# Experts taken in the order of their token counts, two or four to a step, with register-addressed weights

## The chip, the cores and the metric

One core of a Trainium2 chip runs the whole program. The metric is the device time of one launch in microseconds. Its engines are TensorE (PE; its weight loads are listed as PEld), VectorE (DVE), ScalarE (ACT), GpSimd (POOL) and SyncE (SP). All weights are fetched from memory by DMAs that SP issues.

## What the reference computes

Two transformer blocks on 512 tokens of width 1024, in float32. The first has attention and a mixture of experts, the second two kinds of mixing and a dense feed-forward part. The change lies in the mixture of experts:

```python
pg = softmax(hf @ wg + bg); gsel = argmax(pg); pg_sel = max(pg)      # 1 of 4 groups
le = (hf @ we + be).reshape(n, 4, 8)[gsel]                           # 8 experts of that group
p_top, e_loc = top_k(softmax(le), 2)                                 # 2 experts per token
gate = pg_sel * p_top / sum(p_top)
# each of the 32 experts on its tokens:
y = (silu(x @ w1[e]) * (x @ w3[e])) @ w2[e]     # w1, w3: 1024 x 512, w2: 512 x 1024
out[token] += gate * y
```

512 tokens with two experts each are 1024 rows for 32 experts, 32 on average, in numbers that depend on the data. Every expert's weights are 3 x 2 MB, all experts' 201 MB.

## The kernel before

`phase1` does attention. `phase2`, from L835, projects, routes, runs the experts and hands over to the second block (`project2`, `phase3`).

*Routing.* For each of four token tiles `route` finds the two experts. `Ab` marks token and expert. A matmul with a triangle of ones counts, so `rk` (L922) holds a token's place among its expert's tokens, 1 upwards, and 0 where it isn't there; `rt` holds the gates, `rs` their high and low halves. Places make one-hot matrices `G` (L956): column s of an expert is 1 at the token with place s + 1. `gather` (L959) multiplies the normed tokens, held as high and low halves, with `G` and leaves the expert's inputs in `xg`, 64 columns (slots) per expert.

*Steps.* 16 steps (L1052) take two experts each in the order of their numbers. `expert_pair` (L1155) multiplies by `w1` and `w3` (L1174), the first expert's 64 rows of output in partitions 0 to 63, the second's in 64 to 127: each matmul loads 64 columns of `xg` and streams 512 columns of weights. Silu, product and gate (L1181), transposes (L1185), `w2` (L1195). The result goes back to its tokens by a matmul with another one-hot matrix `pm` in the next step (`back`, L1203 to L1210). The list `todo` puts work on the next experts between the parts of a step: in every step half of the next gather, 256 columns wide for two steps, and the two halves of `back`.

*Weights.* `expert` (L179) cuts each matrix into two halves and so issues twelve DMAs of 1 MB per step from SP (L188), into a ring of 14 slots of 1 MB (`NW2`). SP issues in program order; a DMA waits until the matmuls that last read its slot are done. The addresses are fixed, so nothing but slots holds them back: those of step 0 and two of step 1 go out while the routing still runs.

*Leftovers.* An expert with more than 64 tokens is finished by the loop at L1094, one block of 64 slots per pass, with its own gather and weight load. `table` (L1010) lists the blocks; it runs behind step 0.

A scheduler orders the instructions on each engine, by their dependences and place in the source; TensorE, VectorE and SP then work in that order.

Of the kernel before, what the change touches and what calls it, by code (L numbers as in the profile page):

```python
# [20 lines left out]
P = 128  # L21
S = 512
# [7 lines left out]
def constants():  # L30
# [21 lines left out]
    c["iota"] = np.arange(S, dtype=np.float32)[None, :]  # L52
    c["tok1"] = (q[:, None] + P * np.arange(NT)[None, :] + 1).astype(np.float32)
# [18 lines left out]
def packed(I):  # L72
# [5 lines left out]
    for nm, k in ROWS:  # L78
# [7 lines left out]
                        axis=2).reshape(P, -1)], axis=1)  # L86
    c["flat"] = np.concatenate([f(c.pop("iota")), f(I["b_router_g"]), f(I["b_router_e"])])[None]
# [10 lines left out]
DL = 4  # L98


class K:
# [707 lines left out]
    def router_operands(self):  # L809
        nc, I = self.nc, self.I  # L810
        v, gp = nc.vector, nc.gpsimd
        T = lambda shape, nm, dt=F32: self.cp.tile(shape, dt, name=self.name(nm))
        tt, ts = v.tensor_tensor, v.tensor_scalar
        E, CAP = 32, 64
        flat = T([P, S + 36], "flat")
        nc.sync.dma_start(flat, I["flat"].to_broadcast([P, S + 36]))
        iota, br = flat[:, :S], flat[:, S:]
        small = T([P, 28 + 36 * KD], "small")
        nc.sync.dma_start(small, I["small"])
        g2, tok1 = small[:, :KD], small[:, 24:28]  # L820
        self.conds = small[:, 8:24].rearrange("p (i k) -> p i k", i=2)
        w0 = small[:, 28:].rearrange("p (k n) -> p k n", k=KD)
        rt = T([P, NT, 4, 9], "rt")
        for g in range(4):
            gp.tensor_copy(rt[:, :, g, 8], tok1)
# [6 lines left out]
        self.router = iota, iota1, desc, g2, wr, br, rt, tok1, small  # L832


    def phase2(self, p2):  # L835
# [6 lines left out]
        iota, iota1, desc, g2, wr, br, rt, tok1, _ = self.router  # L842

        load = {}
# [5 lines left out]
        weights(0)  # L850
# [4 lines left out]
        rk = T([P, NT, E], "rk")  # L855
        st = T([P, NT, 84], "st")
        rs = T([P, NT, 4, 2, 9], "rs", F32R)
# [26 lines left out]
        def route(t, ps, rstd):  # L884
# [37 lines left out]
            stt(rk[:, t, :], ps[:, 64:64 + E], 1.0, Ab[:, t, :], ALU.add, ALU.mult)  # L922
# [11 lines left out]
            tt(rt[:, t, :, :8], go4, o1[:, None, :].to_broadcast([P, 4, 8]), ALU.mult)  # L934
            v.tensor_copy(rs[:, t, :, 0, :], rt[:, t])
            tt(rs[:, t, :, 1, :], rt[:, t], rs[:, t, :, 0, :].bitcast(F32), ALU.subtract)
# [16 lines left out]

        def onehot(G, u, t):

            tt(G[:, t, :].rearrange("p (e s) -> p e s", e=4), iota1[:, None, :].to_broadcast([P, 4, CAP]),  # L956
               rk[:, t, u * 4:(u + 1) * 4, None].to_broadcast([P, 4, CAP]), ALU.is_equal)

        def gather(xg, G, ks):  # L959
            for k in ks:  # L960
                ps = self.psum()
                for i, (b, t) in enumerate((b, t) for t in range(NT) for b in range(2)):
                    te.matmul(ps[:, :2 * P], hv(t, b)[:, k * P:(k + 1) * P], G[:, t, :],  # L963
                              start=i == 0, stop=i == 2 * NT - 1)
                scaled(xg[:, k, :], ps[:, :2 * P], k)
# [6 lines left out]

        def slots(G, u):

            ps = self.psum()
            for t in range(NT):
                te.matmul(ps[:18, :2 * P], rs[:, t, u // 2].rearrange("p b c -> p (b c)"), G[:, t, :],
                          start=t == 0, stop=t == NT - 1)
            row = T([18, 2 * P], "row")
            sc.activation(row, ps[:18, :2 * P], AF.Copy)  # L980
            yield
            ps = self.psum()
            for j in range(2):
                te.transpose(ps[:, 18 * j:18 * j + 18], row[:, j * P:(j + 1) * P], self.ident[:18, :18])
            pv = ps[:, :36].rearrange("p (j b c) -> p j b c", j=2, b=2)
            cols = T([P, 2, 9], "slot_col")
            v.tensor_copy(cols, pv[:, :, 0, :])
            tt(cols, cols, pv[:, :, 1, :], ALU.add)
            cf = cols.rearrange("p j c -> p (j c)")
            gc = T([P, 2, 2], "gc", bufs=2)  # L990
            e = 4 * (u % 2)
            v.tensor_copy(gc[:64, 0, :], cf[:64, e:e + 12:11])
            v.tensor_copy(gc[64:, 0, :], cf[64:, e + 1:e + 13:11])
            ts(gc[:, 1, :], cf[:, 8:18:9], -1.0, None, ALU.add)
            yield gc

# [3 lines left out]
        for i, (t, n) in enumerate(((0, 0), (0, 1), (1, 0), (1, 1), (2, 1), (3, 1), (2, 0), (3, 0))):  # L1000
            project(t, n)
            if i in (1, 3, 6, 7):
# [3 lines left out]
                onehot(G, 0, t)  # L1006
# [3 lines left out]
        def table():  # L1010

            ps = self.psum()
            for t in range(NT):
                te.matmul(ps[:, :E], self.ones, Ab[:, t, :], start=t == 0, stop=t == NT - 1)
            lim = T([P, NX], "lim")
            ts(lim, iota1[:, :NX], float(CAP), None, ALU.mult)
            more = T([P, 480], "past")[:, :E * NX].rearrange("p (e x) -> p e x", e=E)
            tt(more, ps[:, :E, None].to_broadcast([P, E, NX]), lim[:, None, :].to_broadcast([P, E, NX]), ALU.is_gt)
# [4 lines left out]
            past = T([P, 480], "past").rearrange("p (b e) -> p b e", b=NB)  # L1023
            tt(past, blk[:, 2, None, :].to_broadcast([P, NB, E]), iota[:, :NB, None].to_broadcast([P, NB, E]), ALU.is_le)
            tab = T([P, NB, 2], "tab")
            v.tensor_reduce(tab[:, :, 0], past, AX.X, ALU.add)
            tt(past, past, blk[:, 0, None, :].to_broadcast([P, NB, E]), ALU.mult)
            v.tensor_reduce(tab[:, :, 1], past, AX.X, ALU.add)
            tt(tab[:, :, 1], iota1[:, :NB], tab[:, :, 1], ALU.subtract)
            ts(tab[:, :, 1], tab[:, :, 1], float(CAP), None, ALU.mult)  # L1030
            tabi = T([1, NB + 1], "tabi", I32)
            v.tensor_copy(tabi[:, :NB], tab[:1, :, 0])
# [4 lines left out]
        NB, NX = 15, S // CAP - 1  # L1037
# [4 lines left out]
        part = lambda k: acs[k][:, :2 * P]  # L1042
        for t in range(NT):
            for k in range(KD):
                for b in range(2):
                    te.matmul(part(k), hv(t, b)[:, k * P:(k + 1) * P], G[:, t, :],
                              start=t + b == 0, stop=t + b == NT)
        for k in range(KD):
            scaled(xg[:, k, :], part(k), k)
        _, gc = slots(G, 0)  # L1050
        combine = []
        for i in range(E // 2):  # L1052
            u = i // 2 + 1
            todo = [[] for _ in range(5)]
            j = i % 2
            if 0 < i < E // 2 - 2:
                if i % 2 == 0 or i == 1:
                    nx = new_xg()
                    G = new_G()
                    for t in range(NT):  # L1060
                        onehot(G, u, t)
                    sl = slots(G, u)
                    todo[1].append(lambda s=sl: next(s))
                    got = []
                    todo[3].append(lambda s=sl, g=got: g.append(next(s)))
                    if i == 1:
                        todo[0].append(lambda x=nx, g=G: gather(x, g, range(4)))
                k0 = 4 * j
                todo[2].append(lambda x=nx, g=G, k=k0: gather(x, g, (k, k + 1)))
                todo[3].append(lambda x=nx, g=G, k=k0: gather(x, g, (k + 2, k + 3)))  # L1070
# [4 lines left out]
            weights(i)  # L1075
            w1, w3, w2 = load.pop(i)
            last = i == E // 2 - 1
# [3 lines left out]
            combine = self.expert_pair(T, xg, j * P, w1, w3, w2, gc[:, 0, j:j + 1], gc[:, 1, j:j + 1], iota, todo)  # L1081
# [3 lines left out]
            if j:  # L1085
                xg = nx
                if i < E // 2 - 1:
                    gc, = got
            if i == 0:
                tab, tabi = table()  # L1090


        _, (nb,) = nc.values_load_multi_w_load_instructions(tabi[:, NB:], min_val=0, max_val=NB)
        with tc.For_i(0, nb, 1) as ib:  # L1094
# [5 lines left out]
            pk = T([P, 480], "past")[:, :128].rearrange("p (t g e) -> p t g e", t=NT, g=4)  # L1100
            eq4 = eq.rearrange("p (g e) -> p g e", g=4)
            rv = T([P, NT, 3], "xrv")
            for t in range(NT):
                tt(pk[:, t], rk[:, t, :].rearrange("p (g e) -> p g e", g=4), eq4, ALU.mult)
            v.tensor_reduce(rv[:, :, 0], pk.rearrange("p t g e -> p t (g e)"), AX.X, ALU.add)
            for t in range(NT):
                tt(pk[:, t], rt[:, t, :, :8], eq4, ALU.mult)
# [21 lines left out]
            for f in self.expert_pair(T, xg, 0, w1, w3, w2, gc[:, 0, :1], gc[:, 1, :1], iota):  # L1129
# [25 lines left out]
    def expert_pair(self, T, xg, c0, w1, w3, w2, gate, tok, iota, todo=()):  # L1155
# [4 lines left out]
        ne = len(w1[0])  # L1160
        m = 64 * ne
        rows = [slice(64 * e, 64 * e + 64) for e in range(ne)]
# [6 lines left out]
        for q in range(4):  # L1169
            w, a = (w1, w3)[q // 2][q % 2], ac[q // 2]  # L1170
            for k in range(4):
                for e, r in enumerate(rows):
                    c = c0 + 64 * e
                    te.matmul(a[r, :], xg[:, 4 * (q % 2) + k, c:c + 64], w[e][:, k, :],  # L1174
                              start=q % 2 + k == 0, stop=q % 2 + k == 4)
            if q == 1:
                h = self.hid()
                sc.activation(h[:m], ac[0][:m], AF.Silu)
            elif q < 3:
                between(q // 2)  # L1180
# [571 lines left out]
```

## Time and profile before

| | us |
|---|---|
| three runs | 1564.33, 1557.79, 1564.22 (median 1564.22) |
| profiled execution | 1563.08 |
| its span, first to last instruction | 1561.3 |
| TensorE busy | 1488.0 (95%) |
| VectorE, ScalarE, GpSimd busy | 747.7, 514.7, 124.6 |
| weight DMAs of the experts, first issue to last | 318.3 to 863.8 |
| steps of the experts on TensorE | 372.7 to 903 |

A third of the span is the expert stage. A busy share tells little here, since a matmul in the pipeline counts as busy; what an engine waited for, and the two rates, of TensorE through a step and of the DMA through its bytes, tell more. Granted clock 1.00 is TensorE's higher level, 2.4 GHz, and 0.50 its lower, 1.2 GHz.

### The profile page before, as it was taken

How to read it: one execution, taken by the hardware profiler on the slowest of the kernel's cores; microseconds unless marked ns; L12 is line 12 of the kernel's file. 1: busy time of each engine (PE TensorE's matmuls, PEld its weight loads, DVE VectorE, ACT ScalarE, POOL GpSimd, SP SyncE). 2: the span in 40 equal slices, each digit the busy share in tenths (PEclk: the TensorE clock that was granted, in tenths of full speed). 3: DMA queues.
4: the chain of work that ended last, by engine and by line, in shares of the span. 5: the costliest groups of instructions: out<-in, count | busy, mean ns of one | idle time of the engine just before them, and what ended most of it. 6: DMA issues, size and time to landing. Idle time of an engine off the chain costs nothing. (4 is left out here: it accounts for less than half of the span.)

```text
span 1561.3 us, 19661 instructions
## 1 busy us (share of the span) xinstructions
PE 1488.0 (95%) x7458; PEld 997.8 (64%) x7458; DVE 747.7 (48%) x1891; ACT 514.7 (33%) x1051; POOL 124.6 (8%) x148
## 2 busy tenths in 40 slices
PE   8999999998999999999999979999998999999997
PEld 6777557575444444444443367887878888888886
DVE  5565586775333222223222186767567333325456
ACT  5344453543110010110000064655636222224351
POOL 0021122201000000000000051110101000000000
PEclk9999996999999999999999988999999999999999
DMA  6557750084999999999999611111014213213311
GB/s 244 193 168 211 268 191 30 1 337 170 411 387 368 361 354 381 379 371 374 372 367 378 259 47 38 35 55 55 14 54 175 96 67 108 81 61 115 108 41 54
DMA packets 78129, 303.71 MB, mean 195 GB/s; under 512 B 4896, under 2 KB 10672, under 8 KB 53328
## 3 DMA queue, kind: packets, MB, share of 16 engines
q1 hardware_dynamic: 76192, 298.94, 50.7%
q0 software_dynamic: 1712, 3.35, 0.8%
q8 instruction: 60, 0.98, 0.3%
q14 instruction: 37, 0.30, 0.1%
q10 hardware_dynamic: 128, 0.13, 0.0%
HBM read 297.75 MB, written 2.56 MB: 192 GB/s over the span
## 5 line engine op out<-in xcount | busy, mean ns | idle before, releaser
L1174 PE MATMUL acc<-w,xg 128*64 128x512 f32 x1024 | 255.9, 597 | 0.0
L214 DVE TENSOR_TENSOR wlo<-w,whi 128x512 fp32r<-128x512 f32 (+3 forms) x161 | 104.0, 648 | 209.6 <-ACT whi L213 192.2
L213 ACT ACTIVATE whi<-w 128x512 fp32r<-128x512 f32 (+2 forms) x177 | 104.8, 597 | 221.0 <-PE o L221 87.6
L1174 PEld LDWEIGHTS acc<-w,xg 128*64 128x64 f32 x1024 | 75.5, 137 | 145.6 <-issue 142.5
L1195 PE MATMUL acc<-w,hid 128*64 128x512 f32 x512 | 115.7, 604 | 1.4 <-ACT hid L1187 1.4
L1210 DVE TENSOR_TENSOR x_sb<-ps,x_sb 128x512 f32<-128x512 f32 x128 | 82.0, 686 | 72.6 <-PE ps L1209 72.4
L220 PE MATMUL acc<-whi,hi 128*128 128x512 f32 x280 | 112.9, 406 | 0.4 <-ACT hid L711 0.4
L221 PE MATMUL acc<-wlo,hi 128*128 128x512 f32 x280 | 112.5, 402 | 0.0
L222 PE MATMUL acc<-whi,lo 128*128 128x512 f32 x280 | 111.7, 400 | 0.0
L220 PE MATMUL acc<-hi,whi 128*128 128x512 f32 (+1 forms) x272 | 100.6, 373 | 2.8 <-ACT hi L1607 2.4
L222 PE MATMUL acc<-hi,wlo 128*128 128x512 f32 (+1 forms) x272 | 101.4, 374 | 0.5 <-POOL wlo L214 0.5
L221 PE MATMUL acc<-lo,whi 128*128 128x512 f32 (+1 forms) x272 | 101.2, 373 | 0.2 <-DVE lo L1608 0.2
L1181 DVE SCALAR_TENSOR_TENSOR hid<-acc,gc,hid 128x512 f32<-128x512 f32 x16 | 12.0, 751 | 152.8 <-PE acc L1174 152.8
L1195 PEld LDWEIGHTS acc<-w,hid 128*64 128x64 f32 x512 | 40.3, 138 | 65.0 <-issue 61.3
L220 PE MATMUL ps<-hi,whi 128*128 128x512 f32 x160 | 64.3, 402 | 0.0
L221 PE MATMUL ps<-lo,whi 128*128 128x512 f32 x160 | 64.0, 400 | 0.0
L222 PE MATMUL ps<-hi,wlo 128*128 128x512 f32 x160 | 63.9, 399 | 0.0
L220 PEld LDWEIGHTS acc<-whi,hi 128*128 128x128 f32 x280 | 53.1, 190 | 15.3 <-issue 1.6
L221 PEld LDWEIGHTS acc<-wlo,hi 128*128 128x128 f32 x280 | 53.0, 189 | 13.9 <-issue 2.1
L222 PEld LDWEIGHTS acc<-whi,lo 128*128 128x128 f32 x280 | 53.0, 189 | 13.1 <-issue 0.5
L969 ACT ACTIVATE xg<-ps,small 128x256 f32<-128x256 f32 x29 | 13.8, 475 | 143.7 <-PE ps L963 143.7
L214 DVE TENSOR_TENSOR hid<-acc,hid 128x512 fp32r<-128x512 f32 x16 | 11.1, 691 | 104.4 <-PE acc L1195 104.4
(478 smaller groups left out, 2931.8 us busy)
## 6 DMA issues: line engine op xcount, KB each, us to landing
w<-in_w_dram SPq DMA_DIRECT2D x192, 1024.0 KB
w<-in_w_ada_dram SPq DMA_DIRECT2D x12, 2048.0 KB
w<-in_w_in_dram SPq DMA_DIRECT2D x5, 2048.0 KB
w<-in_w_gate_dram SPq DMA_DIRECT2D x5, 2048.0 KB
w<-in_w_up_dram SPq DMA_DIRECT2D x5, 2048.0 KB
w<-in_w_down_dram SPq DMA_DIRECT2D x4, 2048.0 KB
w<-in_w_o_dram SPq DMA_DIRECT2D x2, 2048.0 KB
w<-in_w_out_dram SPq DMA_DIRECT2D x2, 2048.0 KB
```

The costliest lines, as they stand in the source:

```text
L213: nc.scalar.activation(hi, src, AF.Copy)
L214: (eng or nc.vector).tensor_tensor(lo, src, hi.bitcast(F32), ALU.subtract)
L220: mm(out, a[0], b[0], start=first, stop=False)
L221: mm(out, a[0], b[1], start=False, stop=False)
L222: mm(out, a[1], b[0], start=False, stop=last)
L969: sc.activation(dst, ps, AF.Copy, scale=g2[:, k:k + 1])
L1174: te.matmul(a[r, :], xg[:, 4 * (q % 2) + k, c:c + 64], w[e][:, k, :], start=q % 2 + k == 0, stop=q % 2 + k == 4)
L1181: v.scalar_tensor_tensor(h[:m], ac[1][:m], gate[:m], h[:m], ALU.mult, ALU.mult)
L1195: te.matmul(y[n][r, :], hT[:, k, r], w2[k // 2][e][:, k % 2, n * 512:n * 512 + 512], start=k == 0, stop=k == 3)
L1210: v.tensor_tensor(self.x[:, t, cs], ps, self.x[:, t, cs], ALU.add)
```

## The change

*Order.* Behind the routing `sort` counts the tokens of each expert with a matmul and forms a key: 32 x count + 31 - number, and 65536 more for experts 0 and 1. An expert's rank is the number of larger keys. `PLACES` maps ranks to places: the 16 larger to the steps of two, the 16 smaller to the steps of four. A 64 x 64 permutation `bd` reorders places and gates of all tokens (`rp`) and gives the expert numbers in order (`idi`) and their counts (`cnt`). Step 0 always takes experts 0 and 1, with unsorted places.

*Steps.* 12 of them, 2, 4, 2, 2, 4, 2, 2, 4, 2, 2, 4, 2 experts. A step has 128 slots: 64 for each of two, 32 for each of four. With four, each matmul loads 32 columns of `xg`. Gathers are 128 columns wide for step 0 and the last, else 256 for two steps.

*Weights.* From step 1 on SP reads the expert numbers into registers and addresses the weights by them. In a step of two the pieces are as before. In a step of four a slot holds a quarter of a matrix for two experts, by two DMAs of 512 KB; a step fills 24 slots with 48 DMAs.

*Leftovers.* Blocks start behind 64 or 32 slots; the table is larger (18 blocks), gives a block's first place and its expert's number, and is made in step 2.

```diff
+STEPS = (2, 4, 2, 2, 4, 2, 2, 4, 2, 2, 4, 2)
+_small, _large = iter(range(16, 32)), iter(range(16))
+PLACES = np.array([next(_small if n == 4 else _large) for n in STEPS for _ in range(n)])
...
-            if i < E // 2 and i not in load:
-                load[i] = [self.expert([I[nm][0, 2 * i + a].rearrange("(p k) n -> p k n", p=P) for a in range(2)])
-                           for nm in ("w1", "w3", "w2")]
+            n = STEPS[i]
+            if i:
+                es = [nc.sync.value_load(idi[:, p:p + 1], min_val=0, max_val=E - 1) for p in range(first[i], first[i + 1])]
+            else:
+                es = range(n)
+            out = []
+            for nm in ("w1", "w3", "w2"):
+                if i:
+                    src = [I[nm][0, bass.ds(e, 1)].rearrange("o (p k) n -> p (o k) n", p=P) for e in es]
+                else:
+                    src = [I[nm][0, e].rearrange("(p k) n -> p k n", p=P) for e in es]
+                if n == 2:
+                    out.append(self.expert(src))
+                    continue
+                kq = src[0].shape[1] // 4
+                parts = []
+                for q in range(4):
+                    parts.append([])
+                    for j in range(2):
+                        w = self.slot().rearrange("p (e k n) -> p e k n", e=2, k=kq)
+                        for e in range(2):
+                            nc.sync.dma_start(w[:, e], src[2 * j + e][:, q * kq:(q + 1) * kq, :])
+                            parts[q].append(w[:, e])
+                out.append(parts)
+            return out
...
+        def sort():
+            ps, pt = self.psum(), self.psum()
+            for t in range(NT):
+                te.matmul(ps[:, :E], self.ones, Ab[:, t, :], start=t == 0, stop=t == NT - 1)
+            for t in range(NT):
+                te.transpose(pt[:64, t * P:(t + 1) * P], rt[:, t, :], self.ident)
+            key, col = T([64, 2, E], "key"), T([64, 3], "col")
+            stt(key[:, 0], ps[:64, :E], 32.0, self.order[0][:64], ALU.mult, ALU.add)
+            for i, a in enumerate((key[:, 0], ps[:64, :E])):
+                v.tensor_tensor_reduce(key[:, 1], a, self.own[:64], 1.0, -1.0, ALU.mult, ALU.max, col[:, i:i + 1])
+            ts(key[:, 1], key[:, 0], col[:, 0:1], None, ALU.is_gt)
+            v.tensor_reduce(col[:, 2:3], key[:, 1], AX.X, ALU.add)
+            for h in (slice(0, 32), slice(32, 64)):
+                ts(bd[h, h], self.order[1][h], col[h, 2:3], None, ALU.is_equal)
...
+            for i, a in enumerate((self.expert_of, col[:, 1:2])):
+                te.matmul(ps[:, i * E:(i + 1) * E], a[:E].to_broadcast([E, P]), bd[:E, :E], start=True, stop=True)
+            v.tensor_copy(idi, ps[:1, :E])
...
-        for q in range(4):
-            w, a = (w1, w3)[q // 2][q % 2], ac[q // 2]
-            for k in range(4):
+        for i, (w, a) in enumerate(zip((w1, w3), ac)):
+            kp = KD // len(w)
+            for k in range(KD):
                 for e, r in enumerate(rows):
-                    c = c0 + 64 * e
-                    te.matmul(a[r, :], xg[:, 4 * (q % 2) + k, c:c + 64], w[e][:, k, :],
-                              start=q % 2 + k == 0, stop=q % 2 + k == 4)
+                    te.matmul(a[r, :], xg[:, k, c0 + r.start:c0 + r.stop], w[k // kp][e][:, k % kp, :],
+                              start=k == 0, stop=k == KD - 1)
```

SP's queue behind the twelve pieces of step 0: the last two of them, and then step 1 (`w_3536` on) at once, in the kernel before.

```order
L188 DMA w_2904<-in_w_dram 128x2048
L188 DMA w_2906<-in_w_dram 128x2048
L188 DMA w_3536<-in_w_dram 128x2048
L188 DMA w_3538<-in_w_dram 128x2048
L188 DMA w_3540<-in_w_dram 128x2048
L188 DMA w_3542<-in_w_dram 128x2048
```

In the changed kernel: the last piece of step 0, and then the four expert numbers of step 1 (`TENSOR_LOAD` and two register operations each), and one more register operation ahead of each DMA.

```order
L203 DMA w_2902<-in_w_dram 128x2048
L868 TENSOR_LOAD idi_2906
L868 ISA x2
L868 TENSOR_LOAD idi_2906
L868 ISA x2
L868 TENSOR_LOAD idi_2906
L868 ISA x2
L868 TENSOR_LOAD idi_2906
L868 ISA x2
L888 ISA
L888 DMA w_3695<-in_w_dram 128x1024
L888 ISA
```

What moved: step 1's weights now stand behind loads of `idi`, and are 128 x 1024 pieces.

TensorE between the last gather matmuls of step 0 (`o`) and its first weight matmuls, before.

```order
L1046 MATMUL o_3344<-G_2912,hi_688_3325 128x256
L1046 MATMUL o_3344<-G_2912,lo_689_3326 128x256
L977 MATMUL ps_3417<-G_2912,rs_2911 18x256 x4
L1174 MATMUL acc_3434<-w_2884,xg_3336 64x512
L984 MATMUL ps_3424<-cst,row_3422 128x18 x2
L1174 MATMUL acc_3434<-w_2886,xg_3336 64x512
```

After: the permutation of numbers and counts (L1073) and of places and gates (L1078) stand between them, and the gather is 128 columns wide.

```order
L1141 MATMUL o_3356<-G_2911,hi_695_3337 128x128
L1141 MATMUL o_3356<-G_2911,lo_696_3338 128x128
L1073 MATMUL ps_3429<-bd_2909,small_383 128x32
L1073 MATMUL ps_3429<-bd_2909,col_3321 128x32
L1078 MATMUL ps_3434<-bd_2909,hid_3329 128x64 x4
L1027 MATMUL ps_3444<-G_2911,rs_3440 5x128 x4
L1268 MATMUL acc_3470<-w_2880,xg_3348 64x512
L1033 MATMUL ps_3451<-cst,row_3449 128x5
```

VectorE behind the last tile's places, before: gates, their halves, and the scaling of the gathered `xg`.

```order
L956 TENSOR_TENSOR G_2912<-iota_69_393,rk_2909 128x256
L934 TENSOR_TENSOR rt_385<-st_2910 128x4x8
L935 CAST rs_2911<-rt_385 128x4x9
L936 TENSOR_TENSOR rs_2911<-rt_385,rs_2911 128x4x9
L971 TENSOR_SCALAR xg_3336<-acc_3337,small_383 128x256
L971 TENSOR_SCALAR xg_3336<-acc_3339,small_383 128x256
L971 TENSOR_SCALAR xg_3336<-ps_3341,small_383 128x256
L971 TENSOR_SCALAR xg_3336<-ps_3343,small_383 128x256
L956 TENSOR_TENSOR G_3531<-iota_69_393,rk_2909 128x256 x3
```

After, from the second key operation on: rank, permutation, the same four scalings at half the width, and only then the copy into `idi` that SP's loads wait for.

```order
L1063 ISA key_3320,col_3321<-ps_3310,small_383 64x32
L1063 ISA col_3321 64x1
L1064 TENSOR_SCALAR key_3320<-key_3320,col_3321 64x32
L1065 TENSOR_REDUCE col_3321<-key_3320 64x1
L1067 TENSOR_SCALAR bd_2909<-flat_381,col_3321 32x32 x2
L1014 TENSOR_SCALAR xg_3348<-acc_3349,small_383 128x128
L1014 TENSOR_SCALAR xg_3348<-acc_3351,small_383 128x128
L1014 TENSOR_SCALAR xg_3348<-ps_3353,small_383 128x128
L1014 TENSOR_SCALAR xg_3348<-ps_3355,small_383 128x128
L1074 CAST idi_2906<-ps_3429 1x32
```

What moved: with the first operations on the key (L1061, L1063) and the gates' halves of step 0 (L1022, L1023) ahead of these rows, eleven rows stand between the last gate and the scalings, where there were two.

## Rows read from the trace of the kernel before

**Rows 1.** Waits in the expert stage, 420 to 880 us.

```profile
engine line waited for: us in total, times, longest us
PEld acc L1174 <- issue: 122.1, 416, 0.4
PEld acc L1174 <- DMA w<-in_w_dram: 0.3, 1, 0.3
```

**Rows 2.** Waits of SP's DMA queue in the same stage.

```profile
SPq L188 <- PE acc L1174: 246.6, 98, 7.3
SPq L188 <- PE acc L1195: 129.5, 27, 7.6
```

**Rows 3.** Stretches of the stage, first its header.

```profile
core 0: us, PE busy (x) PEld busy (x) DVE busy (x) ACT busy (x) POOL busy (x), PEclk, DMA share, GB/s
376.75:863.80 487.05, 474.44 (x2201) 209.85 (x2199) 139.46 (x275) 51.73 (x94) 1.72 (x3) 1.00 0.95 376
320.00:350.00 30.00, 27.27 (x151) 22.02 (x149) 23.41 (x96) 14.18 (x29) 1.04 (x1) 1.00 1.00 415
400.00:440.00 40.00, 40.00 (x206) 20.24 (x204) 14.82 (x37) 4.54 (x9) 1.72 (x3) 1.00 1.01 410
377.00:378.00 1.00, 1.00 (x8) 0.40 (x6) 0.00 (x0) 0.00 (x0) 0.00 (x0) 1.00 0.63 98
```

**Rows 4.** Timeline (start, us, instruction): one copy in two steps; the last step.

```profile
523.84 0.60 ACT L1187 ACTIVATE hid<-ps 128x512 f32<-128x512 f32 x1 [7.93 <-PE ps L1185]
557.64 0.60 ACT L1187 ACTIVATE hid<-ps 128x512 f32<-128x512 f32 x1 [7.93 <-PE ps L1185]
888.91 8.83 PE L1195 MATMUL acc<-w,hid 128*64 128x512 f32 x32 [0.69 <-ACT hid L1187]
```

**Rows 5.** Timeline, 64-column and 32-column matmuls in a row.

```profile
406.05 7.09 PE L1174 MATMUL acc<-w,xg 128*64 128x512 f32 x32
165.40 1.92 PE L709 MATMUL acc<-w,cs 128*32 128x512 f32 x16
```

**Rows 6.** Stretches behind the expert stage, and the first matmuls there.

```profile
910.00:920.00 10.00, 8.11 (x28) 6.59 (x29) 10.00 (x31) 7.53 (x17) 3.99 (x3) 0.51 0.26 78
920.00:930.00 10.00, 10.00 (x61) 9.84 (x60) 8.21 (x31) 6.63 (x19) 4.12 (x4) 1.00 0.00 1
910.69 0.69 PE L1595 MATMUL ps<-cst,w 128*128 128x128 f32 x2 [7.69 <-DMA rt<-in_rope_dram]
```

**Rows 7.** The page's packet count.

```profile
DMA packets 78129, 303.71 MB, mean 195 GB/s; under 512 B 4896, under 2 KB 10672, under 8 KB 53328
```

**Rows 8.** Stretches with loads of shorter runs.

```profile
170.00:180.00 10.00, 10.00 (x60) 4.44 (x50) 4.59 (x16) 5.07 (x16) 1.62 (x4) 1.00 1.02 361
908.00:910.00 2.00, 0.00 (x0) 0.00 (x0) 1.96 (x10) 2.00 (x5) 0.75 (x1) 0.50 1.02 422
4.00:12.00 8.00, 5.39 (x17) 3.94 (x17) 5.23 (x11) 5.98 (x11) 0.00 (x0) 1.00 1.03 389
```

**Rows 9.** Timeline around the end of the routing, and SP's queue.

```profile
369.73 0.18 DVE L934 TENSOR_TENSOR rt<-st 128x32 f32<-128x32 f32 x1
371.97 0.28 PE L1046 MATMUL o<-G,lo 128*128 128x256 f32 x1
371.57 0.96 DVE L971 TENSOR_SCALAR xg<-ps,small 128x256 f32<-128x256 f32 x2
376.75 3.76 SPq L188 DMA_DIRECT2D w<-in_w_dram  x3
```

**Rows 10.** SP's weight DMA issues and register load: ns min/median/max.

```profile
L188 SPq DMA_DIRECT2D w<-in_w_dram x192: 327/328/1121, 318.3 to 863.8; - x192
L1093 SPq TENSOR_LOAD <-tabi x1: 495/495/495, 875.9 to 875.9; - x1
L1093 SPq FUSED_REGOPS  x1: 191/191/191, 905.5 to 905.5; - x1
L1093 SPq SEQ_ASSERT  x1: 37/37/37, 905.7 to 905.7; - x1
```

More of the change, by code (lines that the diff above doesn't have):

```diff
@@ L840, in phase2 @@
         E, CAP = 32, 64
-        iota, iota1, desc, g2, wr, br, rt, tok1, _ = self.router
-        load = {}
-        def weights(i):
-            if i < E // 2 and i not in load:
-                load[i] = [self.expert([I[nm][0, 2 * i + a].rearrange("(p k) n -> p k n", p=P) for a in range(2)])
-                           for nm in ("w1", "w3", "w2")]
-        weights(0)
+        iota, iota1, desc, g2, wr, br, tok1, _ = self.router
+        rt = T([P, NT, 64], "rt")
+        first = [0]
+        for n in STEPS:
+            first.append(first[-1] + n)
+        def weights(i):
+            n = STEPS[i]
[23 more added lines that the diff above has]
+            return out
+        load = weights(0)
         ws = self.wos
@@ L952, in spread, with onehot, gather @@
                 stt(r(lo), xk, rstd, r(hi).bitcast(F32), ALU.mult, ALU.subtract)
[L954 to L959, printed above, removed]
+        def onehot(G, steps, t, src):
+            for j, i in enumerate(steps):
+                n = STEPS[i]
+                c = P // n
+                tt(G[:, t, j * P:(j + 1) * P].rearrange("p (e s) -> p e s", e=n),
+                   iota1[:, None, :c].to_broadcast([P, n, c]),
+                   src[:, t, first[i]:first[i + 1], None].to_broadcast([P, n, c]), ALU.is_equal)
+        def gather(xg, G, ks, m):
             for k in ks:
@@ L971, in scaled, with slots @@
                 ts(dst, ps, g2[:, k:k + 1], None, ALU.mult)
-        def slots(G, u):
+        def slots(G, steps, src):
+            p0 = first[steps[0]]
+            n, m = sum(STEPS[i] for i in steps), P * len(steps)
+            rs = T([P, NT, 13], "rs", F32R)[:, :, :2 * n + 1]
+            gates = src[:, :, E + p0:E + p0 + n]
+            v.tensor_copy(rs[:, :, :n], gates)
+            tt(rs[:, :, n:2 * n], gates, rs[:, :, :n].bitcast(F32), ALU.subtract)
+            v.tensor_copy(rs[:, :, 2 * n], tok1)
@@ L975, in slots @@
             ps = self.psum()
             for t in range(NT):
[L977 to L980, printed above, removed]
+                te.matmul(ps[:2 * n + 1, :m], rs[:, t, :], G[:, t, :m], start=t == 0, stop=t == NT - 1)
+            row = T([13, 2 * P], "row")[:2 * n + 1, :m]
+            sc.activation(row, ps[:2 * n + 1, :m], AF.Copy)
@@ L1045, in phase2 @@
                 for b in range(2):
-                    te.matmul(part(k), hv(t, b)[:, k * P:(k + 1) * P], G[:, t, :],
-                              start=t + b == 0, stop=t + b == NT)
+                    te.matmul(part(k), hv(t, b)[:, k * P:(k + 1) * P], G[:, t, :P], start=t + b == 0, stop=t + b == NT)
         for k in range(KD):
[L1049 to L1053, printed above, removed]
-            todo = [[] for _ in range(5)]
[L1055 to L1067, printed above, removed]
+            scaled(xg[:, k, :P], part(k), k)
@@ new lines, in phase2 @@
+        next(order)
+        _, gc = slots(G, (0,), rt)
+        combine, nx, got, over = [], None, [], []
+        N = len(STEPS)
+        for i in range(N):
+            todo = [[] for _ in range(5)]
+            j = (i + 1) % 2
+            ahead = [g for g in (i + 2 - j, i + 3 - j) if g < N] if i else (1, 2)
+            if i == 0 or (j == 0 and ahead):
+                nx = new_xg()
+                G = new_G()
+                for t in range(NT):
+                    onehot(G, ahead, t, rp)
+                sl = slots(G, ahead, rp)
+                todo[1].append(lambda s=sl: next(s))
+                got = []
+                todo[3].append(lambda s=sl, g=got: g.append(next(s)))
+            if ahead:
+                m = P * len(ahead)
+                if i == 0:
+                    todo[0].append(lambda x=nx, g=G, m=m: gather(x, g, range(4), m))
@@ L1074, in phase2 @@
                 todo[4].append(lambda: self.ada_end(T))
-            weights(i)
-            w1, w3, w2 = load.pop(i)
-            last = i == E // 2 - 1
+            if i == 2:
+                todo[4].append(lambda: over.extend(table()))
+            w1, w3, w2 = weights(i) if i else load
+            last = i == N - 1
             if last:
@@ L1084, in phase2 @@
                     f()
-            if j:
+            if j and not last:
                 xg = nx
[L1087 to L1090, printed above, removed]
+                gc, = got
+        tab, tabi = over
         _, (nb,) = nc.values_load_multi_w_load_instructions(tabi[:, NB:], min_val=0, max_val=NB)
```

154 lines of the change are left out of this document (91 added, 63 removed).

## The prediction

> **What bounds the kernel now.** I read the waits of the expert stage first, then the data rate, then one step. TensorE almost never waited for weights there: between 420 and 880 us its weight loads lost 0.3 us to a weight DMA, while SP, which issues the weight DMAs, stood 246.6 + 129.5 = 376 us of 460 waiting for TensorE to finish with a slot [rows 1, 2]. So TensorE sets the pace and the DMA follows. But it follows closely: from 376.75 to 863.80 us the DMA engines were 95% busy at 376 GB/s [rows 3]. Where the queue was full they gave more: 415 GB/s in 320:350 with nothing to wait for and 410 GB/s in 400:440 with TensorE fully at work [rows 3].
>
> The reader is to see two clocks side by side. One step of two experts takes 557.64 - 523.84 = 33.8 us on TensorE [rows 4]; its twelve pieces of 1024 KB (1.0486 MB) take 12.58 MB / 415 = 30.3 us of DMA. The slower one counts, and sixteen steps are paid. And because TensorE is the later one, it still has a whole step to do after the last piece was issued at 863.8: the last down-projection ends at 888.91 + 8.83 = 897.7 us [rows 4].
>
> **The change part by part.** *Steps.* Sixteen steps become twelve, eight of two experts and four of four. The weights stay: 32 experts, 201.3 MB. What TensorE does for a step of two is as before, 33.8 us. A step of four issues twice the weight matmuls, in column tiles of 32 instead of 64. Now 32 such instructions of 64 columns take 7.09 us, 0.222 each; the only 32-column ones in the trace, the 16 of the adaptive-gain product, take 1.92 us, 0.12 each, since four run at a time [rows 5]. A step of four has 128 + 64 of them: 23.0 us at 0.12, where a pair has 64 + 32 at 0.222 = 21.3. With the 33.8 - 21.3 = 12.5 us of everything else (gather, transposes, adding back, gaps) it takes 35.5 us. Without any gain from the narrow tiles it would be 42.6 + 12.5 = 55 us. Its 24 MB take 25.17 MB / 400 = 63 us. So in a step of four TensorE waits for weights either way, and this doubt costs nothing. All twelve steps need about 8 x 33.8 + 4 x 35.5 = 412 us of TensorE, well under what the DMA needs (below). The stage turns from TensorE-bound to DMA-bound, and that is the whole gain: what was 16 x 33.8 us plus a tail becomes bytes divided by rate.
>
> *Is the DMA then always busy?* In two steps of two TensorE falls behind by 2 x (33.8 - 30.3) = 7 us. A step of four leaves it idle in pieces, and then its clock can fall: behind the pause at the end of the stage the granted clock was 0.51 in 910:920, the lower level (1.2 GHz), and 1.00 again in 920:930, with matmuls running from 910.69 [rows 6]. Half speed for 9 us loses 4.5 us. Together 11.5 us behind, against 14 slots x 2.5 us = 35 us that the DMA may run ahead before it finds no free slot. I charge nothing for this within the stage, and if the cover were gone it would cost 4.5 us four times.
>
> *DMA pieces and rate.* Experts 0 and 1 load as before, with static addresses. The other 30 are 188.7 MB: 14 in full pieces (88.1 MB) and 16 in 512 KB halves with runs of 4 KB per partition instead of 8 (100.7 MB). That the present pieces are 8 KB packets is seen from the counts: 78129 - 53328 = 24801 packets of 8 KB and more, and 192 x 128 = 24576 [rows 7]. For full pieces I take 415 (bounds 400, a little over 376/0.95 = 396, and 425). For the halves no row shows this kernel's case. Lower bound: 361 GB/s in 170:180, where only chunks with 2 KB runs move. Upper: 422 in 908:910, a load of 4 KB runs. The first microseconds, 4:12, with 512 KB loads of 4 and 2 KB runs, show 389 [rows 8]. I take 400. Sum: 88.1/415 = 212 us, 100.7/400 = 252 us, 464 us together.
>
> *Where the stream starts.* Before, twelve pieces of step 0 and two of step 1 were loaded ahead, and the stream went on at 376.75 when the first slots came free. Now nothing of step 1 may be issued until the order is known: two pieces, 5 us of DMA, move behind that point (they are in the 188.7 MB). The last routing write of before ends at 369.73 + 0.18 = 369.9 [rows 9]. Behind it come eleven small VectorE operations at about 0.18 us, to 371.9; the permutation matmul stands behind the gather matmuls of step 0, which end near 372.2 now and as they are half as wide not later; four half-size scalings (0.48 us each at full size) stand ahead of the integer copy on VectorE: about 373.3. Then SP reads four expert numbers, each at 0.495 + 0.191 + 0.037 = 0.72 us by the one such load in the trace [rows 10], 2.9 us: 376.2, and one register operation and an issue, 0.19 + 0.33: 376.7. By luck that is where the stream began before. Then as now the flow begins about a microsecond after the issue (98 GB/s in 377:378) [rows 3]: 378. Bounds: 2 us earlier, if the operations overlap more, 6 us later. Step 0 itself starts about 1.3 us later on TensorE (order and permutation matmuls ahead of it); the DMA hides that.
>
> *Issue on SP.* Register addresses add an operation per DMA, and halves double their number: 84 + 192 = 276 issues instead of 180, at 0.33 + 0.19 = 0.52 us: 143 us on SP over 464, hidden. The program gives its DMAs eight completion semaphores in turn, so eight can be out, and the loads of expert numbers (2 or 4 x 0.72 us) lie under at least 8 x 0.5 MB = 10 us of queued transfer. The longest issue of before was 1.12 us [rows 10]; at that, 309 us, still hidden.
>
> *The rest.* Gathers fall from 8 to 7, of which two half as wide, and the adding back from 16 times to 12: work of an engine that now waits, worth nothing. The table of leftover blocks grows to some 15 VectorE operations of up to 576 columns and moves to step 2, under TensorE's slack; if not hidden, about 10 us once. The three later stages are the same instructions.
>
> **Sum.** 378 + 464 = 842 us for the last weight byte. Behind it stands only the second half of the last down-projection, 16 instructions, 3.6 us at full clock, 7.1 at half; I take 6: 848 us, instead of 897.7. Gain 49.7 us. From the profiled execution's 1563.1 us (span 1561.3; the median of the runs shown is 1564.22, 0.07% off) that is 1513 us.
>
> Two statements of the Trainium skill speak against this sum; nothing above rests on them. DMA: Bandwidth & Descriptors, section "Where 436 GB/s comes from", says that HBM-to-SBUF transfers are held to about 358 GB/s by one core's share of the memory; an estimate by that page is 527 us for the 188.7 MB, and no gain. Here 410 and 415 GB/s stand over 40 and 30 us [rows 3], so the trace disagrees. The same page, section "Measured (HBM→SBUF, 128 partitions, SWDGE, issued from GpSimd)", wants at least 1 MiB per DMA for 75% of peak, and its section "Anatomy of one DMA" gives each DMA a fixed 2 us: an estimate of 164 GB/s for a lone 512 KB DMA. The 389 GB/s of 4:12 [rows 8] come from loads of 512 KB, many at a time and issued by SP, so the fixed part overlaps there; whether it does with register addresses no row shows.
>
> **The rivals.** *The halves are slow.* If 4 KB runs move no faster than 2 KB ones, 361 GB/s: 100.7/361 = 279 us instead of 252, end at 875, gain 23, 1540 us. For it: 361 is a measured row. Against: 389 and 422 in the other two.
>
> *The whole stream is held at a ceiling.* If the memory can't sustain over a whole stage more than the 361 GB/s row, 188.7/361 = 523 us, end 907, 9 us later than before: 1572 us, slower. For it: long-run rates in the stage were only 376. Against: SP waited for TensorE there, and 410 held for 40 us. (The page's 358 GB/s would be this rival.)
>
> *SP becomes the bound.* If a register-addressed issue costs far more than a static one: 276 issues beat the old end when each takes over (897.7 - 6 - 377)/276 = 1.86 us; at 2.1 us the stage ends at 963 and the time is 1628. From 1.68 us on (464/276) it decides. For it: no row of before shows such an issue. Against: it needs over five times the static 0.33, and three times with the register operation.
>
> *The leftover loop runs.* The order is worth its price only if the 16 emptier experts hold at most 32 tokens each and the others 64. The loop after the steps, L1094, ran no pass before: 192 weight DMAs are 16 x 12 and L188 shows no more [rows 10]. The reference's router on its inputs gives 18 to 51 tokens per expert, with experts 0 and 1 kept in front the sixteen fuller ones end at 31 and the emptier ones begin at 30: no leftover. If the inputs were others, a pass costs a weight load with nothing beside it (6.29 MB, 15 us) and some 30 us of matmuls one expert at a time: one pass 1558, two passes 1603.
>
> **How the numbers follow.** My case has 0.77, slow halves 0.10, the ceiling 0.05, SP 0.04, leftovers 0.04 (half of that one pass, half two). No change is within 0.5%, 7.8 us, about what a measurement of this kernel can tell. The first two are faster, 0.87, and of the ceiling a milder form (380 GB/s or so) is faster too, 0.01: 0.88. Same: one leftover pass and a part of the ceiling, 0.04. Slower 0.08. Range: fast end 88.1/425 + 100.7/420 = 447 us, end 829, 1494 us; slow end the halves at 361 and a start 4 us late, 1544. I give 1494 to 1544.
>
> **What would show it.** Right: TensorE's weight loads wait for weight DMAs for 50 us and more, nearly all in the four wide steps; SP waits for DMA lanes rather than for TensorE; the DMA share is near 1.00 from 378 to about 842 at 400 to 415 GB/s; 16 wide weight matmuls in 1.9 us; the first register load near 373; the last down-projection ends within 10 us of the last weight byte, with the granted clock below 1 in parts of the wide steps. Wrong: a DMA share well under 1 while SP is busy issuing (SP), a share of 1 at under 380 GB/s (ceiling, halves), weight DMAs beyond 12 x 8 + 48 x 4 = 288, or the stage ending where it did.

## The result and the profile after

The changed kernel takes 1517.03 us (median of four runs, 1516.21 to 1519.38) against 1562.23 (four runs, 1557.79 to 1564.33): ratio 0.9717, 95% interval 0.9690 to 0.9743. The forecast was 1513. The profiled execution takes 1516.21 us, 46.9 less than the 1563.08 of before. The expert stage accounts for it: the last down-projection ends at 842.51 + 8.83 = 851.3 instead of 897.7, and the first matmul behind the stage starts at 864.28 instead of 910.69 [rows 4, 6], 46.4 us earlier both times.

Stretches of the stage after the change, with the columns of [rows 3]:

```profile
355.00:380.00 25.00, 21.59 (x101) 19.02 (x103) 16.24 (x77) 5.83 (x12) 3.38 (x2) 0.50 0.04 10
380.00:390.00 10.00, 10.00 (x54) 5.50 (x52) 2.30 (x13) 0.95 (x2) 0.00 (x0) 0.89 0.94 352
390.00:400.00 10.00, 10.00 (x49) 3.36 (x46) 0.63 (x4) 2.25 (x3) 0.00 (x0) 1.00 0.79 286
...
565.00:610.00 45.00, 43.58 (x185) 17.99 (x182) 11.49 (x31) 4.91 (x9) 0.00 (x0) 1.00 1.02 421
620.00:690.00 70.00, 66.68 (x340) 25.34 (x339) 13.26 (x38) 5.85 (x11) 0.00 (x0) 1.00 1.02 410
700.00:735.00 35.00, 33.77 (x154) 14.73 (x152) 9.26 (x18) 3.60 (x7) 0.00 (x0) 1.00 1.01 421
740.00:805.00 65.00, 61.97 (x323) 24.36 (x322) 12.10 (x25) 5.05 (x10) 0.00 (x0) 1.00 1.02 410
```

In the stretches from 565 on the DMA share is 1.01 to 1.02; before it was 0.95 over the stage [rows 3]. Stretches mostly of full pieces (565:610, 700:735) run at 421 GB/s, those mostly of halves (620:690, 740:805) at 410. A half is both smaller (512 KB) and in shorter runs (4 KB); the two are not parted here. Two rows at the start are below that, 390:400 above all, behind a stretch with TensorE's clock at its lower level. The Trainium skill's page DMA: Bandwidth & Descriptors, section "Where 436 GB/s comes from", holds HBM loads to about 358 GB/s per core; this trace, in which one core runs alone, disagrees over more than 400 us.

Waits of SP's DMA queue, 370 to 850:

```profile
SPq L888 <- DMA w<-in_w_dram: 142.8, 158, 2.6
SPq L203 <- DMA w<-in_w_dram: 118.0, 79, 2.5
SPq L868 <- DVE left L1100: 46.4, 1, 46.4
SPq L888 <- PE acc L1268: 15.8, 14, 6.2
...
SPq L888 <- PE acc L1290: 7.6, 3, 6.1
```

Before, SP stood 376 us waiting for TensorE [rows 2]; now it waits 261 us for earlier weight DMAs and some 31 for TensorE, of which the two lines shown are 23. The 46.4 us are the wait for the first expert number; they begin at 329, when step 0's pieces have been issued. TensorE's weight loads, 380 to 850, and then two of its groups in a timeline:

```profile
PEld acc L1268 <- DMA w<-in_w_dram: 20.6, 29, 2.2
PEld acc L1290 <- DMA w<-in_w_dram: 10.7, 35, 1.0
```

```profile
448.99 5.41 PE L1290 MATMUL acc<-w,hid 128*32 128x512 f32 x48
...
678.77 17.27 PE L1290 MATMUL acc<-w,hid 128*32 128x512 f32 x64
```

The first group shows the price of 32-column matmuls: 5.41/48 = 0.113 us each. The second is a whole down-projection of a step of four at 0.27 each. At 0.113 it would take 7.2 us, so it lost some 10, and they count as busy. Its weight loads wait ten times for a weight DMA, mostly 1.28 us apart, which is what 512 KB take at 410 GB/s. So the weights set its pace, but the view of waits puts only 3.5 us down to them.

SP's register work (ns min/median/max), and the end of the stage:

```profile
L888 SPq FUSED_REGOPS  x192: 37/46/56, 377.9 to 805.6; - x192
L888 SPq MOVE w<-in_w_dram x192: 29/29/38, 378.0 to 805.7; - x192
L888 SPq DMA_DIRECT2D w<-in_w_dram x192: 332/333/1107, 378.1 to 806.4; - x192
L868 SPq TENSOR_LOAD <-idi x30: 261/269/481, 375.4 to 807.4; - x30
...
L203 SPq DMA_DIRECT2D w<-in_w_dram x96: 328/333/627, 316.0 to 826.6; - x96
```

```profile
836.51 3.65 PE L1268 MATMUL acc<-w,xg 128*64 128x512 f32 x14 [1.32 <-DMA w<-in_w_dram]
841.07 0.75 PE L1279 MATMUL ps<-cst,hid 128*128 128x128 f32 x4 [0.91 <-DVE hid L1275]
842.51 8.83 PE L1290 MATMUL acc<-w,hid 128*64 128x512 f32 x32 [0.69 <-ACT hid L1281]
...
864.28 1.97 PE L1690 MATMUL ps<-cst,w 128*128 128x128 f32 x8 [7.68 <-DMA flat<-in_rope_dram]
```

A register-addressed issue costs 0.046 + 0.029 = 0.08 us of register work and 0.33 of issue. There are 96 + 192 = 288 weight DMAs, none of a leftover pass.

### The profile page after: what moved, and what is told of

It is laid out like the page before. It is cut to its first block, busy times and chain, and to the rows that moved or that the text cites. A ratio compares the mean times of both kernels' runs of the same rounds, so it can differ in the third digit from the quotient of the medians.

```text
span 1514.4 us, 20068 instructions
## 1 busy us (share of the span) xinstructions
PE 1432.1 (95%) x7322; PEld 962.0 (64%) x7322; DVE 720.6 (48%) x1907; ACT 502.1 (33%) x1031; POOL 123.8 (8%) x145
## 5 line engine op out<-in xcount | busy, mean ns | idle before, releaser
L1268 PE MATMUL acc<-w,xg 128*32 128x512 f32 (+1 forms) x1024 | 216.1, 601 | 3.9 <-DMA w<-in_w_dram 3.9
L1268 PEld LDWEIGHTS acc<-w,xg 128*32 128x32 f32 (+1 forms) x1024 | 56.9, 124 | 122.8 <-issue 98.4
L1290 PE MATMUL acc<-w,hid 128*32 128x512 f32 (+1 forms) x512 | 120.8, 607 | 0.8 <-ACT hid L1281 0.7
L1290 PEld LDWEIGHTS acc<-w,hid 128*32 128x32 f32 (+1 forms) x512 | 37.8, 125 | 72.7 <-issue 59.3
L1305 DVE TENSOR_TENSOR x_sb<-ps,x_sb 128x512 f32<-128x512 f32 x96 | 60.6, 684 | 22.9 <-PE ps L1304 22.7
L235 PEld LDWEIGHTS acc<-hi,whi 128*128 128x128 f32 x272 | 51.0, 189 | 14.9 <-ACT hi L1702 3.0
```

Source lines behind the costliest of these rows:

```text
L235: mm(out, a[0], b[0], start=first, stop=False)
L1268: te.matmul(a[r, :], xg[:, k, c0 + r.start:c0 + r.stop], w[k // kp][e][:, k % kp, :], start=k == 0, stop=k == KD - 1)
L1290: te.matmul(y[n][r, :], hT[:, k, r], w2[k // kp][e][:, k % kp, n * 512:n * 512 + 512], start=k == 0, stop=k == 3)
L1305: v.tensor_tensor(self.x[:, t, cs], ps, self.x[:, t, cs], ALU.add)
```

## The experiments

Each ratio is to runs of the kernel before on the same chip. Their medians were 1561.4 to 1562.7 us in all sets, so times of different sets can be compared within some 1.3 us. The first four ask what bounded the stage.

**Steps of two, sorted.** `STEPS = (2,) * 16` and `PLACES = np.arange(32)`.

> All sixteen steps of two, experts still sorted on the chip and addressed by register; nothing else changed. My theory (before, a step of two was bound by TensorE at about 33 us; the change gains only because four experts share one TensorE step): the gain is gone, and the later start of step 0 stays, so 1562 plus 3 to 12: 1565 to 1574 us, with SyncE waiting for TensorE again. Rival (the gain is from the sorted order, the register addresses or another placement of the transfers): 1545 or less.

1580.7 us, ratio 1.0118 (1.0086 to 1.0150): the gain is gone, so sorting and registers gain nothing. SP waits for TensorE again, 248.3 + 102.3 us of the 460 from 420 on. It is slower than either theory said; its steps take 34.5 us (transposes copied at 532.90, 567.32, 601.81), not 33.8, for a reason that stays open.

**Half the bytes in the steps of four.** In `weights`:

```
-  w = self.slot()...        # for j in range(2)
+  if j: parts[q] += parts[q][:2]; continue
```

> The four steps of four load two of their four experts and use each twice: 50.3 MB fewer (four times 12.6 MB) with the same work on TensorE, VectorE and ScalarE; the output is not the reference's. My theory (the stage is bound by the transfers now): it falls until TensorE bounds it: 8 steps of 33.8 and 4 of 35.5 are 412 us from 377, so the last down-projection ends near 800 instead of 851, and the time is 1460 to 1480. Rival (TensorE or its chain of waits still bounds it): 1517 plus or minus 8.

1453.6 us, 63 less than the changed kernel, a little under the range. The last down-projection ends at 782.37 + 7.14 = 789.5: that is the expectation's own 377 + 412, though it says near 800. Bytes set the time of the changed kernel. With half of them in the wide steps TensorE does: SP waits 244 us for it from 370 to 850.

**More TensorE work in the steps of four.** `for rep in range(2 if ne == 4 else 1)` around the w1 and w3 matmuls.

> In the four steps of four, the products with w1 and w3 are accumulated twice over: 64 more 32-column matmuls for each step, in sixteens of 1.9 us, so 7.6 us of TensorE in each, 30 us in all; the output is not the reference's. My theory (transfers bound the stage, TensorE has some 17 us to spare in each group of 2, 4, 2): 1514 to 1523 us. Rival (TensorE bounds it): 1547.

1517.4 and 1525.6 us (mean granted clock 0.973 and 0.963), where the changed kernel gave 1516.2 at 0.971 and 1519.4 at 0.966. One of the two runs lies above the theory's range, the median 1521.5 within it: most or all of the 30 us are hidden.

**Before, with half its bytes.** In `expert`: `if out[i]: out[i].append(out[i][0]); continue`.

> The kernel before, with one expert of each pair loaded and used for both: half of the 201 MB of weights, the same work on every engine; the output is not the reference's. My theory (before, TensorE bounded this stage): 1550 to 1566 us, no change or little. Rival (the stage was already bound by the transfers, and the change gained by spreading them better): 1520 or less.

1510.5 and 1516.8 us: 49 us gone by the medians, where I expected nothing; the time is the rival's. Its steps take 30.27 us (transposes copied at 514.04, 544.33, 574.58). But TensorE's order had changed too: with fewer loads the scheduler kept the written order. In the kernel before, products that add the previous step back (L1209) and gathers (L963) had been put between the weight products, so that these ran in runs of 2, 14, 2 and 46; in the half-bytes kernel in 16, 32 and 16. Order or bytes? The next pair decides.

**Before, in the written order, all bytes loaded.** With the names of classes shortened:

```
+  pe = [a for a in nc.cur_bb.bb.instructions[mark:] if a.engine == te.engine]
+  for a, b in zip(pe, pe[1:]):
+      tc.add_manual_dep(b, a.name, DependencyInfo(NoSync, DATA), reason="order")
```

> The kernel before, all its weights loaded, with TensorE's instructions of the middle steps held in the order in which the code writes them (order-only dependencies; the order that the half-bytes kernel has): the w1 and w3 products in runs of 8, 16 and 8 rows, not 1, 7, 1 and 23 with the scatter and gather products between them. Theory A (the 33.8 us of a step of two were not all work: 3.5 us went to the broken order, as the half-bytes kernel's 30.3 us with the other order suggests): a step takes 30.3 to 31, 12 to 13 steps save 3 us each, 1518 to 1530 us. Theory B (the half-bytes kernel gained because its weights were there sooner): the order changes nothing, 1555 to 1565.

1523.2 us, ratio 0.9751 (0.9726 to 0.9776): theory A. The first part of a step on TensorE, of before and then of this kernel: the w1 and w3 products, of the products that add back only the first group, and the transposes:

```profile
600.86 1.89 PE L1209 MATMUL ps<-hid,pm 128*128 128x512 f32 x6
602.69 1.07 PE L1174 MATMUL acc<-w,xg 128*64 128x512 f32 x2
...
605.86 3.65 PE L1174 MATMUL acc<-w,xg 128*64 128x512 f32 x14
...
610.10 1.07 PE L1174 MATMUL acc<-w,xg 128*64 128x512 f32 x2
...
613.20 10.51 PE L1174 MATMUL acc<-w,xg 128*64 128x512 f32 x46
624.62 0.75 PE L1185 MATMUL ps<-cst,hid 128*128 128x128 f32 x4 [0.91 <-DVE hid L1181]
```

```profile
588.61 3.60 PE L1180 MATMUL acc<-w,xg 128*64 128x512 f32 x16
592.14 2.25 PE L1215 MATMUL ps<-hid,pm 128*128 128x512 f32 x8
594.32 7.09 PE L1180 MATMUL acc<-w,xg 128*64 128x512 f32 x32
...
603.52 3.65 PE L1180 MATMUL acc<-w,xg 128*64 128x512 f32 x16
609.09 0.65 PE L1191 MATMUL ps<-cst,hid 128*128 128x128 f32 x4
```

And eight steps of each, grouped (busy, mean ns of one, idle before); before, 523.84 to 794.92:

```profile
L1174 PE MATMUL acc<-w,xg 128*64 128x512 f32 x512 | 130.4, 597 | 0.0
...
L1185 PE MATMUL ps<-cst,hid 128*128 128x128 f32 x32 | 6.0, 309 | 7.3 <-DVE hid L1181 7.3
```

the written order, 518.96 to 761.12:

```profile
L1180 PE MATMUL acc<-w,xg 128*64 128x512 f32 x512 | 114.8, 595 | 0.0
...
L1191 PE MATMUL ps<-cst,hid 128*128 128x128 f32 x32 | 5.2, 286 | 0.0
```

The same 512 matmuls take 15.6 us less. A lone pair of 64-column matmuls costs 1.07 us, where two in a long run cost 2 x 0.22, and it came twice in a step. The transposes wait 0.91 us where no gather stands ahead of them. Together 15.6 + 7.3 + 0.8 = 23.7 of the 271.1 - 242.2 = 28.9 us, and 3.6 more lie in the products that add back. The account is rough, since the busy times of neighbouring groups overlap. A step then takes 242.2/8 = 30.27 us, which is also 12.58 MB at 416 GB/s. The same stretch of the kernel before and of this one, and this one's waits of SP from 420 to 880:

```profile
490.00:560.00 70.00, 68.17 (x321) 30.99 (x321) 20.36 (x40) 7.99 (x15) 0.00 (x0) 1.00 0.92 364
490.00:560.00 70.00, 70.00 (x349) 31.30 (x350) 21.95 (x44) 8.72 (x16) 0.00 (x0) 1.00 1.01 415
```

```profile
SPq L188 <- PE acc L1180: 202.5, 53, 5.3
SPq L188 <- PE acc L1201: 134.9, 27, 7.6
```

In this one TensorE and the DMA are both full. SP still waits for TensorE, and the half-bytes kernel has the same step of 30.27 us at a DMA share of 0.63 (560:620): 30.27 is TensorE's own time, and the DMA's lies just beside it. The half-bytes kernel is some 10 us faster than this one, with the same step; what lies outside these steps was not parted.

**After, in the written order.** The same edit to the changed kernel.

> The changed kernel with TensorE's instructions held in the written order in the same way, and nothing else. Theory (the stage is bound by the stream of weights from 380 to 845, whatever TensorE's order): 1514 to 1520. Rival (TensorE's order costs here too, some 3 us in each of 12 steps): 1480 to 1500. Rival on the other side (TensorE waits in place on weights that the free order would have filled with other work, and frees room later): 1522 to 1530.

1517.4 us (1514.6 to 1522.9), ratio 0.9722 (0.9696 to 0.9749): no change. Where bytes set the time, as here, TensorE's order is free.

The others look for what is left at the start and in the rate.

**Static addresses.** `es = range(first[i], first[i + 1])` in every step.

> The changed kernel, with every expert's weights addressed by a constant (the place, not the sorted number), so that SyncE reads no number and waits for no sort; the sort itself and all else stay; the weights belong to other experts than the gathered tokens do, so the output is not the reference's. My theory: only the room for about two pieces is free before step 0 releases its own, so those 2 MB come 5 us earlier and the time falls by 2 to 6: 1511 to 1515. Rival 1 (the 30 register loads, 0.44 us each, stand in the stream): 13 less, about 1504. Rival 2 (the pieces wait for step 0's room in any case): 1517 plus or minus 2.

1515.7 us, 0.9685 (0.9667 to 0.9702), just above the theory's range and within rival 2's; 1510.5 and 1510.9 at a mean clock of 0.974, 1515.7 to 1518.1 at 0.966 and 0.967. The 13 us of rival 1 are not there. In the profile the two pieces beyond step 0 are loaded ahead, and the next weight DMA is issued at 389.69, when step 0, whose products began at 383.92, has given room (SP's longest wait for these products is 43.5 us): the order isn't what holds the stream back. Whether 2 us are gained is within the clock's effect.

**Numbers first.** `next(order)` ahead of the gather of step 0.

> The product that puts the experts' numbers in sorted order stands ahead of the last part of step 0's gather in place of behind it, so that the numbers are there near 370 and not 375.4. Theory: the first transfer of the stream moves from 378 to some 372, but only two pieces have room, so 2 MB are gained, 2 to 5 us: 1512 to 1515. Rival 1: the product waits for the sort on VectorE and holds step 0's gather back by 1 to 2 us: 1518 to 1519. Rival 2: the stream waits for step 0's room all the same, 1517 plus or minus 2.

1518.3 us, 0.9715 (0.9701 to 0.9728): no gain. The first issue follows the last routing matmul by 6.8 us (372.52 to 379.33) instead of 12.1 (365.98 to 378.08). But step 0's products start 12.1 us behind that matmul (384.57), no sooner than before the edit (11.5), and up to 420 SP waits 18.1 us for them instead of 12.2: rival 2.

**Step 0's gather at 256 columns.** `onehot(G, (0, 0), t, rt)` and `G[:, t, :2 * P]`.

> Step 0's gather and its one-hot columns at the width of before (256 columns, the second 128 a repeat that nothing reads): 64 matmuls of 0.12 us instead of 0.11. Theory: the granted clock fell to 0.50 from 355 on because TensorE had less to do there; with the width of before it falls later and rises sooner (0.82 in 365 to 370, as before), step 0 starts near 373 instead of 377.5, its room comes free some 6 us sooner, and the time falls to 1510 to 1514. Rival: the clock falls all the same (the waits for routing are the reason), the wider matmuls at half clock and the one-hot work cost 3 to 6 us: 1520 to 1523.

1510.1 us, 0.9688 (0.9662 to 0.9714), in two groups: 1509.1 to 1510.1 at a mean clock of 0.976 to 0.978, 1516.9 and 1518.7 at 0.970 and 0.968. Of the first group is the profile:

```profile
355.00:380.00 25.00, 20.27 (x128) 15.58 (x128) 18.23 (x87) 6.16 (x13) 3.48 (x3) 0.86 0.18 61
390.00:400.00 10.00, 10.00 (x64) 6.17 (x62) 4.34 (x21) 1.55 (x3) 0.00 (x0) 1.00 1.02 408
```

With the clock at 0.86 in place of 0.50 step 0's products start 6.8 us behind the last routing matmul (365.96 to 372.77), not 11.5, and the starved stretch is gone. The profiled executions take 1509.1 and 1516.2 us, and the 7 us stand at both ends of the stage: the first and the last step's transposes are copied at 395.30 and 834.51, in the changed kernel at 402.24 and 841.86. So half clock through step 0 costs about 7 us. That the slower runs of this kernel lost the clock there too is likely by their mean clock, but none of them was profiled.

**Whole pieces.** `self.expert(src)` for every step.

> The steps of four loaded in whole pieces (1 MB for one expert, 8 KB at a stretch) as the steps of two are, 96 transfers in the place of 192. Theory (the stage is bound by the rate of the stream; 512 KB transfers ran at 410 GB/s, 1 MB ones at 421): 100.7 MB take 239 instead of 246 us, so 1510 to 1513. Rival (room comes free more coarsely, and TensorE starts on 4 MB instead of 2 MB of a weight): 1519 to 1526.

1507.8 us, 0.9671 (0.9648 to 0.9694), 9 us less by the median and below the theory's range; the five runs go from 1507.2 (mean clock 0.969) to 1515.4 (0.961). The wide stretches now run at 421 GB/s too, and 100.7 MB at 421 instead of 410 explain 6.4 us. In the profile the last step's transposes are copied 6.3 us earlier (835.58). The other 3 lie behind that and were not separated.

**Both, and both with wider products in the routing.** First the last two edits together, then in the gather `G[:, t, None, :2 * P].to_broadcast([P, 2, 2 * P])` for the first three tiles.

> The changed kernel with whole 1 MB pieces in the steps of four and step 0's gather at 256 columns, both. Theory: the two gains add where the clock holds through step 0: 7 from the start (stream from 375, no starved stretch at 390 to 400) and 7 to 9 from the faster pieces: 1500 to 1504; where the clock falls in the routing all the same, 1508 to 1512. Rival (the two share one cause): 1507 to 1510.

> Whole pieces and the 256-column gather as in the run before this, and the first three token tiles' gather products 512 columns wide (the same columns twice; the second half is read by nobody): 48 matmuls of 0.23 instead of 0.12 us between 350 and 366, where TensorE waits for the routing. Theory (the granted clock falls because TensorE has too little to do there, and the fall costs 7 us): the clock stays up, step 0 starts at 373 to 375, 1500 to 1504 us in all five runs. Rival (the fall comes from the waits themselves, or the wider products hold the routing back): 1506 to 1512.

The first: 1508.8 us, 0.9654 (0.9631 to 0.9676), no better than whole pieces alone. The mean clock of its runs is 0.965 to 0.970, and in the profile it is 0.73 from 355 to 380. That fits the theory's case of a clock that falls all the same, and the rival as well. The second: 1503.0 us, 0.9634 (0.9616 to 0.9653), runs from 1500.6 at 0.983 to 1508.4 at 0.967: inside the theory's range by the median, but not all five. It is 14 us faster than the changed kernel. Two stretches of its fastest run:

```profile
355.00:380.00 25.00, 21.62 (x116) 15.06 (x116) 19.23 (x91) 6.66 (x15) 4.67 (x3) 0.93 0.05 9
...
620.00:690.00 70.00, 60.43 (x333) 23.18 (x330) 14.53 (x41) 5.98 (x11) 0.00 (x0) 1.00 1.01 421
```

## Why the prediction was right, and where it was not

- *TensorE-bound becomes DMA-bound.* Right in what it said of the time. SP's waits turned round, the share is 1.02, and adding work to TensorE or taking bytes away shows the new bound from both sides.
- *"What TensorE does for a step of two is as before, 33.8 us."* That was the step as it ran, not the work in it: 3.6 us were the price of the order. The prediction took a busy engine that nobody kept waiting for an engine doing only needed work, and so had no rival that removes the bound without larger steps. That other way brings 38 us where the change brought 45. The page Perfetto Trace Analysis of the Trainium skill, section "Identifying the Most-Contended Engine", warns that matmul busy time is not a good measure of how close a kernel is to the roofline. These runs agree: TensorE counts as 97% busy in 490:560 of the kernel before, with steps of 33.9 us, and as 100% busy in the written order, with steps of 30.3 us for the same work.
- *Rates.* Right. 415 was 421, 400 was 410: 209 + 246 = 455 us instead of 464, 9 us better.
- *Start.* 376.7 was 378.1; SP's numbers and issues were cheaper than taken, but the integer copy came 2 us later, behind products at half clock. Not foreseen were the clock at 0.50 from 355 to 380 and step 0, whose transposes are copied at 402.24, 12.6 us later than before (389.60). I let the DMA hide that delay; it can't, since step 0 holds twelve of the fourteen slots. To 400 the stream moved 6.4 MB where 20 us at 415 are 8.3: 4.6 us lost beside 2 us of later flow.
- *End.* By the bytes of the stretches the last weight byte comes near 841 (842 forecast). *"Behind it stands only the second half of the last down-projection"* failed: the whole of it does, 8.83 us from 842.51 on, since the products before it wait for weights up to 836.51. So it is 10 us and not 6.
- *Sum.* -9 for the rates, +2 and +5 at the start, +4 at the end: 848 + 2, near the 851.3 measured. That the forecast came within 4 us is luck in part: the better rates paid for the start and the end.
- *Signs.* Of the 50 us and more that TensorE's weight loads were to wait for weights, the view lists 20.6 + 10.7 = 31; more lies inside groups that count as busy (17.27 us for the work of 7.2). As a sign it was badly chosen. The clock was to fall in the wide steps; in 620:690 and 740:805 it is 1.00.
- *Rivals.* Slow halves, ceiling, SP's issue and leftovers: none came. The halves do cost, some 9 us, but at 410 GB/s and not at 361.

Two things stay open. One is how much of the 45 us the larger steps bring beyond an order that costs nothing: beside the reordered kernel before, the change is 1523.2 - 1517.0 = 6 us faster, but the runs of the two nearly touch (1520.6 and 1519.4), and the two also start differently. The other is why one run keeps the clock through the start and another of the same kernel doesn't.

## What to carry to other kernels

When an engine is busy all the time, compare its step with the sum of its instructions in long runs, and look at the order before its work is cut: here a lone pair cost more than twice its share. Where the times of two engines for a step lie near each other, as the DMA's 30.3 us and TensorE's 33.8 (30.3 in the written order) here, price both with one experiment each. And a stream that depends on slots starts when the first user gives them back, so that user's own delay, its clock included, belongs in the sum.

## What was not expected

The scheduler's order depends on the loads, so an edit of the bytes also edits TensorE: a step of 33.8 us became one of 30.3. A register-addressed weight DMA costs SP only 0.08 us of register work more than a static one, where the prediction took 0.19. One and the same kernel differs by up to 10 us from run to run (1509.1 to 1518.7 with step 0's gather at 256 columns), in step with its mean clock (0.978 to 0.968).
